# The gated delta rule in chunks of 128 tokens, with the transposed inverse of a level by transposing

## The chip, the cores and the metric

The kernel runs on one core of one Trainium2 chip. The metric is the device time of one launch in microseconds (us); the median of several executions is compared. The core has a matrix engine (TensorE, PE, with its weight loads listed as PEld), a vector engine (VectorE, DVE), a scalar engine (ScalarE, ACT), GpSimd (POOL) and SyncE (SP), which issues the DMAs here. The engines run their own queues in order and wait for each other by semaphores.

## The reference

The program is two blocks on 512 tokens of width 1024. The first is a depth-2 transformer-like block. The second has, beside a dilated window attention, a gated delta rule of 4 heads of width 128, which is what the change touches. Cut to that:

```python
def gated_delta_rule_chunked(q, k, v, g, beta):
    """S_t = exp(g_t) (I - beta_t k_t k_t^T) S_{t-1} + beta_t k_t v_t^T,  o_t = S_t^T q_t."""
    ...                                   # q, k, v, g, beta cut into chunks of CHUNK = 64
    gc = jnp.cumsum(g, axis=-1)           # within a chunk
    decay = jnp.exp(jnp.where(causal, gc[..., :, None] - gc[..., None, :], -jnp.inf))
    kb = k * beta[..., None]
    lower = jnp.where(strict, jnp.einsum('bhnid,bhnjd->bhnij', kb, k) * decay, 0.0)
    tmat = lax.linalg.triangular_solve(eye + lower, ...)        # the inverse
    u = jnp.einsum('bhnij,bhnjd->bhnid', tmat, v * beta[..., None])
    w = jnp.einsum('bhnij,bhnjd->bhnid', tmat, kb * jnp.exp(gc)[..., None])
    a_intra = jnp.where(causal, jnp.einsum('bhnid,bhnjd->bhnij', q, k) * decay, 0.0)

    def step(S, inp):                     # one chunk after the other
        qi, ki, ui, wi, ai, gci = inp
        v_new = ui - jnp.einsum('bhck,bhkv->bhcv', wi, S)
        o = jnp.einsum('bhck,bhkv->bhcv', qi * jnp.exp(gci)[..., None], S) + jnp.einsum('bhij,bhjv->bhiv', ai, v_new)
        glast = gci[..., -1]
        S = S * jnp.exp(glast)[..., None, None] + jnp.einsum(
            'bhck,bhcv->bhkv', ki * jnp.exp(glast[..., None] - gci)[..., None], v_new)
        return S, o
```

The size of a chunk is free: the recurrence in the docstring has the same answer for each.

## The kernel before

Everything is recorded first and then ordered by a planner (`Program.order`): it gives each instruction a guessed cost (`cost`, line 364), keeps a clock per engine, and takes for each engine the earliest-recorded instruction that can start, so that work recorded later fills the gaps of work recorded earlier. All instructions are issued from one line (684), so the names of tiles tell them apart. The planner also moves some elementwise work between DVE, POOL and ACT. `SLOW` is a table of guessed costs for the scan's products.

Large products are done as three single-pass products of high and low halves; the products of the delta rule are float32, which the profile lists as two instructions each. 512 tokens are four tiles `t` of 128; a tile named here has 128 partitions and 4 x 128 columns, one block for each `t`.

`block2` (line 1863) makes the second block: one head of the delta rule after the other (`dn_head`, line 1542), then the window attention (`swa`), a merge and the output product. For a head:
- `dnp` projects q, k, v and a gate; a convolution (`cy`), a silu (`sth`, `feat`) and norms follow, with transposes (`dtr`, a product with the identity).
- `gps` is the running sum of g over a chunk, `egl` its exponent at the end of a chunk. ET and E hold the decays, L the lower triangle, LT its transpose.
- The inverse of I + L is built by levels: D is the inverse of blocks of size s, DT its transpose. A level multiplies the part of LT between two blocks (LmT, by a mask `lvT`) with D, copies that to X, and subtracts X times DT from DT and DT times X from D. Five levels, with masks s = 2 to 32, give blocks of 64. The lines are 1652 to 1665; `mm4` does four products, one for each `t`.
- The scan goes over 8 chunks: `p1` is wT times the state S, `vn` is u minus p1, `dno` collects the output (a part from S by qeT, a part from vn by aT), `p2` is kd times vn and S is renewed with it. The trace lists p1 and p2 as p. Since a chunk has 64 tokens, the products use 64 rows or columns of the array: 128*64, 64*64 and 64*128 tiles.

Heads overlap: while a head runs its levels and scan, PE projects the next head (`dnp`), and behind the last heads the attention's projections (`pj`).

Of the kernel before, what the change touches and what calls it, by code (L numbers as in the profile page):

```python
# [10 lines left out]
F32 = mybir.dt.float32  # L11
F32R = mybir.dt.float32r
AF = mybir.ActivationFunctionType
OP = mybir.AluOpType
# [5 lines left out]
NEG = -1e30  # L20
# [40 lines left out]
def block_consts():  # L61
    f = np.float32
    p = np.arange(128)
    i, j = p[:, None], p[None, :]
    same = (i // 64) == (j // 64)
    U = (same & (i <= j)).astype(f)
    Bc = same.astype(f)
    causT = np.where(same & (j >= i), 0.0, NEG).astype(f)
    strict = (same & (i > j)).astype(f)

    def lv(s):
        return ((i // (2 * s) == j // (2 * s)) & (i % (2 * s) >= s) & (j % (2 * s) < s)).astype(f)
    lvT = np.stack([lv(s).T for s in (2, 4, 8, 16, 32)], 1)
    cur = np.where(j <= i, 0.0, NEG).astype(f)
    prev = np.where(j >= i, 0.0, NEG).astype(f)
    g2 = np.where((j <= i) & ((i - j) % 4 == 0), 0.0, NEG).astype(f)
    inv = (f(500000.0) ** (-np.arange(0, 32, 2, dtype=f) / f(32))).astype(f)
    ang = np.arange(TX, dtype=f)[:, None] * inv[None, :]
    c, s = np.cos(ang).astype(f), np.sin(ang).astype(f)
    C, S = np.concatenate([c, c], 1), np.concatenate([-s, s], 1)  # L80
    tabs = []
    for x in (C, S):
        tabs.append(np.stack([x.reshape(4, 128, 32).transpose(1, 0, 2), x.reshape(128, 4, 32)], 1))
    return [("U", U), ("Bc", Bc), ("causT", causT), ("strict", strict), ("nm0", -lv(1)), ("nm0T", -lv(1).T),
            ("lvT", lvT), ("cpc", np.concatenate([cur, prev, cur], 1)), ("g2", g2),
            ("cos", tabs[0]), ("sin", tabs[1]), ("e", np.full((128, 16), np.e, f))]
# [270 lines left out]
        return call  # L357

SLOW = {"p1": 0.27, "dno": 0.33, "p2": 0.42}


def cost(eng, fn, args, kw, n):

    views = [x for x in args if isinstance(x, View)]
    if eng == "sync":
        nbytes = 4 * int(np.prod([x.shape for x in args if hasattr(x, "shape")][0]))
        return max(nbytes / 360e3, 0.43), 2.2
    if eng == "tensor":  # L370
        if fn == "transpose":
            return 0.109, 0.1
        lhs, rhs = args[1], args[2]
        if rhs.dtype == F32:
            c = max(4 * n / 2400, 0.213) + 0.005
            if "tile_position" in kw:
                c /= 3.8
            elif args[0].tile.name in SLOW:
                c = SLOW[args[0].tile.name]
            elif lhs.shape[-1] == 64:  # L380
                c *= 0.63
            return c, 0.25
        return max(n * 0.000434 + 0.0095, 0.112), 0.12
    psum = any(v.tile.space == PSUM for v in views)
    ptrs = sum(isinstance(x, View) and x.shape[1:] == (1,) for x in args[2:] + (kw.get("scale"), kw.get("bias"))) if n > 1 else 0
    if eng == "vector":
        each = 0.0063 if fn == "reciprocal" else 0.00052 if fn == "tensor_scalar" and not psum else 0.00104
        return 0.07 + 0.06 * ptrs + n * each, 0.06
    if eng == "scalar":
        return 0.051 + 0.042 * (not psum) + 0.093 * (ptrs + ("accum_out" in kw)) + n * 0.000833, 0.06  # L390
    if kw.get("op") == OP.pow:
        return 0.3 + 0.165 * n, 0.1
    if fn == "memset":
        return 0.05 + n * 0.0004, 0.1
    slow = fn == "tensor_scalar" and isinstance(args[2], View)
    return 0.12 + n * (0.0025 if slow else 0.0022 if fn != "tensor_scalar" else 0.0009), 0.1
# [294 lines left out]
class Net:  # L691
# [337 lines left out]
    def swiglu(self, ws, z, n, ah, al, order="1657243"):  # L1029


        nc = self.nc
        X, Y, Z = (self.bank("gu")[:, :n] for _ in range(3))
        m1, u2, u3, g0 = (self.t2("gu")[:, :n] for _ in range(4))
        add = nc.vector.tensor_add
        for i in (int(x) for x in order):
            ps = {1: X, 2: X, 6: Y, 7: Y, 4: Y, 5: Z, 3: Z}[i]
            self.mm3(ps, [(ws[i][k], tuple(x[:, k] for x in z[i])) for k in range(4)], ((0, 0), (1, 0), (0, 1)),
# [5 lines left out]
            elif i == 6:  # L1044
                add(u2, m1, Y)
            elif i == 7:
                add(u3, m1, Y)
                add(u3, u3, Z)
            elif i == 4:
                add(m1, m1, Y)  # L1050
                nc.vector.tensor_mul(g0, g0, m1)
# [434 lines left out]
    def dn_stats(self, M, C, Pm):  # L1486
# [40 lines left out]
        gf = g.rearrange("p a b -> p (a b)")  # L1527
        nc.tensor.matmul(ps[:, 0, :], C["U"], gf, start=True, stop=True)
        nc.tensor.matmul(ps[:, 1, :], C["Bc"], gf, start=True, stop=True)
# [12 lines left out]
    def dn_head(self, h, M, C, Pm, st, ones):  # L1542
        nc = self.nc
# [4 lines left out]
        def t2(nm):  # L1548
            return self.t24(nm)

        def flat(x):
            return x.rearrange("p a b -> p (a b)")

        def bc(col):
            return col.unsqueeze(2).to_broadcast([128, 4, 128])

        def bt(m):
            return m.unsqueeze(1).to_broadcast([128, 4, 128])
# [5 lines left out]
        for i in range(4):  # L1564
            ps = self.bank("dnp")
            self.mm3(ps, [(ws[i][k], (zh[:, k, 0:TX], zl[:, k, 0:TX])) for k in range(KD)])
            dst = t2("feat")
            if i < 3:
# [3 lines left out]
                for j in (2, 1, 0):  # L1572
                    s = 3 - j
                    nc.vector.scalar_tensor_tensor(y[:, s:], ps[:, :TX - s], cw[:, j:j + 1], y[:, s:],
                                                   op0=OP.mult, op1=OP.add)
# [6 lines left out]
        def transposes(src):  # L1582
            tr = self.bank4("dtr")
            for t in range(4):
                nc.tensor.transpose(tr[:, t, :], src[:, t, :], ident)
            return tr

        def mm4(l, r):
            ps = self.bank4("dmm")
            for t in range(4):  # L1590
                nc.tensor.matmul(ps[:, t, :], l[:, t, :], r[:, t, :], start=True, stop=True)
            return ps
# [15 lines left out]
        rg = t2("rg")  # L1608
        nc.gpsimd.tensor_tensor(rg, bt(C["U"]), bc(gh), op=OP.mult)
        gps = self.bank4("gps")  # L1610
        nc.tensor.matmul(flat(gps), ones, flat(rg), start=True, stop=True)
        egl = self.sm.tile([128, 4, 2], F32, tag="egl", name="egl")
        nc.scalar.activation(egl, gps.rearrange("p t (c i) -> p t c i", c=2)[:, :, :, 63], AF.Exp)
        ET = t2("ET")
        nc.vector.tensor_tensor(ET, gps, bc(st["ngc"][:, h]), op=OP.add)
        nc.gpsimd.tensor_tensor(ET, ET, bt(C["causT"]), op=OP.add)
# [10 lines left out]
        for t in range(4):  # L1627
            nc.vector.scalar_tensor_tensor(L[:, t, :], G[:, t, :], st["beta"][:, h, t:t + 1], E[:, t, :],
                                           op0=OP.mult, op1=OP.mult)
        LT = t2("LT")  # L1630
        nc.scalar.copy(LT, transposes(L))
        D_, DT = t2("D"), t2("DT")
# [7 lines left out]
        aT = t2("aT")  # L1640
# [3 lines left out]
        qeT = t2("qeT")  # L1644
# [4 lines left out]
        kbe, kd = t2("kbe"), t2("kd")  # L1649
        nc.gpsimd.tensor_tensor(kbe, kn, bc(st["bge"][:, h]), op=OP.mult)  # L1650
        nc.gpsimd.tensor_tensor(kd, kn, bc(st["edl"][:, h]), op=OP.mult)
        for li in range(5):
            LmT = t2("LmT")
            nc.gpsimd.tensor_tensor(LmT, LT, bt(C["lvT"][:, li, :]), op=OP.mult)
            X = t2("X")
            nc.scalar.copy(X, mm4(LmT, D_))
            YT = mm4(X, DT)
            if li < 4:
                Y = mm4(DT, X)
                D2 = t2("D")  # L1660
                nc.vector.tensor_sub(D2, D_, Y)
                D_ = D2
            DT2 = t2("DT")
            nc.vector.tensor_sub(DT2, DT, YT)
            DT = DT2
        u, wT = t2("u"), t2("wT")
        nc.scalar.copy(u, mm4(DT, vb))
# [1 line left out]

        o = self.bank4("dno")  # L1670
        S = None
        for c in range(8):
            t, p0 = c // 2, 64 * (c % 2)
            ps = slice(p0, p0 + 64)
            if S is None:
                vn, vt = u, t
            else:
                p1 = self.bank("p1")[:, 0:128]
                nc.tensor.matmul(p1[ps, :], wT[:, t, ps], S, start=True, stop=True)
                vn, vt = M.tile([128, 1, 128], F32, tag="vn", name="vn", bufs=2), 0  # L1680
                nc.vector.tensor_sub(vn[ps, 0, :], u[ps, t, :], p1[ps, :])
                nc.tensor.matmul(o[ps, t, :], qeT[:, t, ps], S, start=True, stop=False)
            nc.tensor.matmul(o[ps, t, :], aT[ps, t, ps], vn[ps, vt, :], start=S is None, stop=True)
            if c < 7:
                p2 = self.bank("p2")[:, 0:128]
                nc.tensor.matmul(p2, kd[ps, t, :], vn[ps, vt, :], start=True, stop=True)
                S2 = M.tile([128, 128], F32, tag="S", name="S", bufs=2)
                if S is None:
                    nc.vector.tensor_copy(S2, p2)
                else:  # L1690
                    nc.vector.scalar_tensor_tensor(S2, S, egl[:, t, c % 2:c % 2 + 1], p2, op0=OP.mult, op1=OP.add)
                S = S2
        sq = t2("osq")
        nc.scalar.activation(sq, o, AF.Square)
# [394 lines left out]
```

## Time and profile before

| | |
|---|---|
| median of 3 runs | 3343.21 us (3342.05 to 3347.4) |
| the profiled execution | 3345.79 us, span 3344.0 us |
| mean granted clock of PE | 0.991 |
| PE busy | 98% of the span |
| DVE, ACT, POOL busy | 70%, 40%, 8% |
| DMA engines, q1 | 30.0% of the span, 334.61 MB |

The span is the time from the first to the last instruction of the profiled execution. In a timeline row the first number is the start, the second the busy time to the end of the last instruction of the row; matmuls are pipelined, so the difference between two starts, not the busy time, is what a row takes of PE. Tile shapes of PE stand as rows*columns of the array, then the shape that is written. A line such as `PE dmm L684 <- DVE D L684` reads: PE, about to write dmm, waited for DVE's write of D.

### The profile page before, as it was taken

What the parts mean: (1) busy time and instruction counts of PE and PEld (TensorE: products, weight loads), DVE (VectorE), ACT (ScalarE), POOL (GpSimd) and SP (SyncE); (2) the same over time, 40 slices, a digit from 0 to 9 for tenths busy, and PEclk for the clock granted to TensorE, in tenths of its full rate; (3) what the DMA queues carried; (4) which work ended last, traced back from release to release, by engine and by line L of the source; (5) the groups of instructions that cost most, each with busy time, mean ns of one, the idle gap of its engine ahead of it and who ended that gap; (6) DMA issues with size and microseconds to landing.
All of it is one profiled execution on the core that took longest, in us unless ns stands there. A gap on an engine that the chain in (4) does not pass through costs nothing.

```text
span 3344.0 us, 47695 instructions
## 1 busy us (share of the span) xinstructions
PE 3263.3 (98%) x18310; PEld 2812.8 (84%) x18310; DVE 2356.4 (70%) x4547; ACT 1341.6 (40%) x2764; POOL 268.3 (8%) x285
## 2 busy tenths in 40 slices
PE   7999999999999999999999999998999999999999
PEld 4889998777788999969999989767999887798987
DVE  6567769786766777887777795668889885666333
ACT  5333334554442333354333354345444442334431
POOL 1000001112000000110000012000000111321000
PEclk9999999999999999999999999998999999999999
DMA  7342113222543212352121232253333511112231
GB/s 254 108 170 70 65 68 127 86 89 102 180 157 115 75 58 75 111 187 73 63 75 59 91 118 88 98 189 101 102 107 108 167 57 45 51 45 66 82 95 63
DMA packets 161524, 337.66 MB, mean 101 GB/s; under 512 B 12256, under 2 KB 57696, under 8 KB 161168
## 3 DMA queue, kind: packets, MB, share of 16 engines
q1 hardware_dynamic: 161296, 334.61, 30.0%
q8 instruction: 144, 2.36, 0.3%
q14 instruction: 84, 0.69, 0.1%
HBM read 316.69 MB, written 17.87 MB: 100 GB/s over the span
## 4 chain that ended last, share of the span: by engine, by line
PE 85%; DVE 8%; DMA 3%; ACT 2%; issue 1%; SPq 0%; POOL 0%; POOLq 0%; ACTq 0%; DVEq 0%
PE gu L684 33%; PE dn L684 18%; PE pj L684 13%; PE pjf L684 5%; DVE h L684 2%; PE dnp L684 2%; PE ada L684 2%; PE dmm L684 2%; PE tr L684 1%; PE fin L684 1%; PE yb L684 1%; PE sc L684 1%; DMA raw<-in_ada_w 1%; PE pv L684 1%; PE ptr L684 1%
## 5 line engine op out<-in xcount | busy, mean ns | idle before, releaser
L684 ACT CAST whi<-raw 128x512 fp32r<-128x512 f32 x885 | 522.3, 620 | 673.1 <-PE gu L684 206.1
L684 DVE TENSOR_TENSOR wlo<-raw,whi 128x512 fp32r<-128x512 f32 x848 | 561.3, 687 | 223.2 <-ACT whi L684 210.1
L684 DVE TENSOR_TENSOR gu<-gu 128x384 f32<-128x384 f32 (+1 forms) x616 | 321.5, 522 | 276.8 <-PE gu L684 261.2
L684 DVE TENSOR_TENSOR h<-h,dn 128x512 f32<-128x512 f32 x404 | 273.6, 681 | 75.6 <-PE dn L684 74.7
L684 PE MATMUL dn<-wlo,ah 128*128 128x512 f32 x968 | 309.6, 394 | 0.0
L684 PE MATMUL dn<-whi,ah 128*128 128x512 f32 x968 | 308.8, 396 | 0.3 <-ACT ah L684 0.3
L684 PE MATMUL dn<-whi,al 128*128 128x512 f32 x968 | 304.9, 395 | 0.0
L684 PE MATMUL gu<-zh,whi 128*128 128x384 f32 (+1 forms) x1408 | 288.9, 326 | 13.1 <-DVE gu L684 7.4
L684 PE MATMUL gu<-zh,wlo 128*128 128x384 f32 (+1 forms) x1408 | 287.4, 322 | 0.0
L684 PE MATMUL gu<-zl,whi 128*128 128x384 f32 (+1 forms) x1408 | 283.2, 322 | 0.0
L684 PEld LDWEIGHTS gu<-zh,whi 128*128 128x128 f32 x1408 | 237.6, 189 | 36.8 <-DVE gu L684 8.7
L684 PEld LDWEIGHTS gu<-zh,wlo 128*128 128x128 f32 x1408 | 237.0, 189 | 0.9 <-issue 0.8
L684 PEld LDWEIGHTS gu<-zl,whi 128*128 128x128 f32 x1408 | 235.6, 189 | 1.0 <-issue 0.8
L684 PE MATMUL gu<-zxh,wlo 128*128 128x384 f32 (+1 forms) x1056 | 218.9, 326 | 5.2 <-DVE wlo L684 5.2
L684 ACT CAST whi<-ws 128x512 fp32r<-128x512 f32 x176 | 106.2, 620 | 280.1 <-PE dn L684 229.2
L684 PE MATMUL gu<-zxh,whi 128*128 128x384 f32 (+1 forms) x1056 | 214.6, 327 | 0.9 <-DVE gu L684 0.7
L684 PEld LDWEIGHTS dn<-wlo,ah 128*128 128x128 f32 x968 | 182.1, 188 | 39.5
L684 PE MATMUL gu<-zxl,whi 128*128 128x384 f32 (+1 forms) x1056 | 215.2, 325 | 0.0
L684 PEld LDWEIGHTS dn<-whi,al 128*128 128x128 f32 x968 | 181.8, 188 | 38.8 <-DVE al L684 0.2
L684 PEld LDWEIGHTS dn<-whi,ah 128*128 128x128 f32 x968 | 179.8, 189 | 39.1 <-ACT whi L684 3.4
L684 PE MATMUL pj<-whi,zh 128*128 128x512 f32 (+1 forms) x848 | 202.2, 373 | 8.2 <-ACT whi L684 3.1
L684 PEld LDWEIGHTS gu<-zxh,whi 128*128 128x128 f32 x1056 | 180.2, 189 | 18.8 <-ACT whi L684 4.7
(390 smaller groups left out, 5292.1 us busy)
## 6 DMA issues: line engine op xcount, KB each, us to landing
raw<-in_ffn_gu SPq DMA_DIRECT2D x176, 512.0 KB
raw<-in_ada_w SPq DMA_DIRECT2D x144, 512.0 KB
raw<-in_ffn_w_down SPq DMA_DIRECT2D x88, 512.0 KB
raw<-in_w_in SPq DMA_DIRECT2D x72, 512.0 KB
raw<-in_od_w_in SPq DMA_DIRECT2D x16, 512.0 KB
raw<-in_ev_w_in SPq DMA_DIRECT2D x14, 512.0 KB
gate<-gate SPq DMA_DIRECT2D x10, 512.0 KB
raw<-in_ev_w_out SPq DMA_DIRECT2D x8, 512.0 KB
```

The source lines that it names most:

```text
L684: getattr(self.real[o.eng], o.fn)(*[real(x) for x in o.args], **{k: real(v) for k, v in o.kw.items()})
```

## The change

A chunk has 128 tokens: the masks (`U`, `Bc`, `causT`, `strict`) cover whole blocks of 128, a sixth level with s = 64 is added, and the scan has four steps on whole tiles. In a level DT is no longer reduced by a product of its own: D is reduced, transposed on PE (`dtr`) and copied to DT by ACT; only the last level, which needs DT alone, still has the product with DT. The packed constants grow from 2448 to 2576 columns. The planner's `SLOW` table goes, so it guesses the scan's products like others.

```diff
     i, j = p[:, None], p[None, :]
-    same = (i // 64) == (j // 64)
-    U = (same & (i <= j)).astype(f)
-    Bc = same.astype(f)
-    causT = np.where(same & (j >= i), 0.0, NEG).astype(f)
-    strict = (same & (i > j)).astype(f)
+    U = (i <= j).astype(f)
+    Bc = np.ones((128, 128), f)
+    causT = np.where(j >= i, 0.0, NEG).astype(f)
+    strict = (i > j).astype(f)
...
-    lvT = np.stack([lv(s).T for s in (2, 4, 8, 16, 32)], 1)
+    lvT = np.stack([lv(s).T for s in (2, 4, 8, 16, 32, 64)], 1)
...
-SLOW = {"p1": 0.27, "dno": 0.33, "p2": 0.42}
...
-            elif args[0].tile.name in SLOW:
-                c = SLOW[args[0].tile.name]
...
-        egl = self.sm.tile([128, 4, 2], F32, tag="egl", name="egl")
-        nc.scalar.activation(egl, gps.rearrange("p t (c i) -> p t c i", c=2)[:, :, :, 63], AF.Exp)
+        egl = self.sm.tile([128, 4], F32, tag="egl", name="egl")
+        nc.scalar.activation(egl, gps[:, :, 127], AF.Exp)
...
-        for li in range(5):
+        for li in range(6):
             LmT = t2("LmT")
             nc.gpsimd.tensor_tensor(LmT, LT, bt(C["lvT"][:, li, :]), op=OP.mult)
             X = t2("X")
             nc.scalar.copy(X, mm4(LmT, D_))
-            YT = mm4(X, DT)
-            if li < 4:
-                Y = mm4(DT, X)
+            DT2 = t2("DT")
+            if li < 5:
                 D2 = t2("D")
-                nc.vector.tensor_sub(D2, D_, Y)
+                nc.vector.tensor_sub(D2, D_, mm4(DT, X))
                 D_ = D2
-            DT2 = t2("DT")
-            nc.vector.tensor_sub(DT2, DT, YT)
+                nc.scalar.copy(DT2, transposes(D_))
+            else:
+                nc.vector.tensor_sub(DT2, DT, mm4(X, DT))
             DT = DT2
...
-        for c in range(8):
-            t, p0 = c // 2, 64 * (c % 2)
-            ps = slice(p0, p0 + 64)
-            if S is None:
-                vn, vt = u, t
-            else:
+        for t in range(4):
+            vn = u[:, t, :]
+            if S is not None:
                 p1 = self.bank("p1")[:, 0:128]
-                nc.tensor.matmul(p1[ps, :], wT[:, t, ps], S, start=True, stop=True)
-                vn, vt = M.tile([128, 1, 128], F32, tag="vn", name="vn", bufs=2), 0
-                nc.vector.tensor_sub(vn[ps, 0, :], u[ps, t, :], p1[ps, :])
-                nc.tensor.matmul(o[ps, t, :], qeT[:, t, ps], S, start=True, stop=False)
-            nc.tensor.matmul(o[ps, t, :], aT[ps, t, ps], vn[ps, vt, :], start=S is None, stop=True)
-            if c < 7:
+                nc.tensor.matmul(p1, wT[:, t, :], S, start=True, stop=True)
+                vn = M.tile([128, 128], F32, tag="vn", name="vn", bufs=2)
+                nc.vector.tensor_sub(vn, u[:, t, :], p1)
+                nc.tensor.matmul(o[:, t, :], qeT[:, t, :], S, start=True, stop=False)
+            nc.tensor.matmul(o[:, t, :], aT[:, t, :], vn, start=S is None, stop=True)
+            if t < 3:
                 p2 = self.bank("p2")[:, 0:128]
-                nc.tensor.matmul(p2, kd[ps, t, :], vn[ps, vt, :], start=True, stop=True)
+                nc.tensor.matmul(p2, kd[:, t, :], vn, start=True, stop=True)
                 S2 = M.tile([128, 128], F32, tag="S", name="S", bufs=2)
                 if S is None:
                     nc.vector.tensor_copy(S2, p2)
                 else:
-                    nc.vector.scalar_tensor_tensor(S2, S, egl[:, t, c % 2:c % 2 + 1], p2, op0=OP.mult, op1=OP.add)
+                    nc.vector.scalar_tensor_tensor(S2, S, egl[:, t:t + 1], p2, op0=OP.mult, op1=OP.add)
                 S = S2
```

The planner orders the instructions anew from the first level of head 0 on; ahead of it PE's order is the same. PE at the first two levels of head 0, before (`dnp` are projections of head 1, in three kinds by the halves that they multiply):

```order
L684 MATMUL dmm<-D,LmT 128x128 x4
L684 MATMUL dnp<-zh,whi 128x512 x8
L684 MATMUL dmm<-DT,X 128x128 x4
L684 MATMUL dmm<-X,DT 128x128 x4
L684 MATMUL dnp<-zl,whi 128x512 x8
L684 MATMUL dnp<-zh,wlo 128x512
L684 MATMUL dmm<-D,LmT 128x128 x4
L684 MATMUL dnp<-zh,wlo 128x512 x7
```

and now:

```order
L677 MATMUL dmm<-D,LmT 128x128 x4
L677 MATMUL dnp<-zh,whi 128x512 x8
L677 MATMUL dmm<-X,DT 128x128 x4
L677 MATMUL dnp<-zl,whi 128x512 x8
L677 MATMUL dnp<-zh,wlo 128x512
L677 MATMUL dtr<-constA,D 128x128 x4
L677 MATMUL dmm<-D,LmT 128x128 x4
L677 MATMUL dnp<-zh,wlo 128x512 x7
L677 MATMUL dnp<-zh,whi 128x512 x2
```

The second product of the level (written as `dmm<-DT,X`) is gone, and four transposes of D stand ahead of the next level's first product, with eight or nine projections before and behind the level's second product.

PE in the scan of head 0, before (the number behind p tells its buffers apart), the fourth of eight steps and the start of the fifth:

```order
L684 MATMUL p_27026<-S,wT 64x128
L684 MATMUL dno<-S,qeT 64x128
L684 MATMUL dnp<-zh,wlo 128x512 x5
L684 MATMUL dno<-vn,aT 64x128
L684 MATMUL p_27041<-vn,kd 128x128
L684 MATMUL dnp<-zh,whi 128x512 x7
L684 MATMUL p_27055<-S,wT 64x128
L684 MATMUL dno<-S,qeT 64x128
```

and now, the second of four steps and the start of the third:

```order
L677 MATMUL p_27012<-S,wT 128x128
L677 MATMUL dno<-S,qeT 128x128
L677 MATMUL dnp<-zl,whi 128x512 x6
L677 MATMUL dnp<-zh,wlo 128x512
L677 MATMUL dno<-vn,aT 128x128
L677 MATMUL p_27030<-vn,kd 128x128
L677 MATMUL dnp<-zh,wlo 128x512 x7
L677 MATMUL p_27043<-S,wT 128x128
L677 MATMUL dno<-S,qeT 128x128
```

The products write 128 rows where they wrote 64 (p2 always wrote 128), there are half as many steps, and a step has up to 14 projections where it had 12.

## Rows read from the trace of the kernel before

**Rows 1.** The page: busy us, share of the span and instructions of each engine.

```profile
PE 3263.3 (98%) x18310; PEld 2812.8 (84%) x18310; DVE 2356.4 (70%) x4547; ACT 1341.6 (40%) x2764; POOL 268.3 (8%) x285
```

**Rows 2.** Windows: length, busy us of PE, PEld, DVE, ACT, POOL, clock, DMA.

```profile
2689.00:3000.00 311.00, 307.25 (x1739) 251.85 (x1738) 199.34 (x393) 100.89 (x199) 73.56 (x88) 1.00 0.14 43
...
3057.00:3090.00 33.00, 27.83 (x126) 23.91 (x125) 24.98 (x40) 13.64 (x44) 2.08 (x3) 0.84 0.25 80
```

**Rows 3.** Waits of PE, 2689 to 3057 us: total, times, longest.

```profile
PE dmm L684 <- DVE D L684: 1.7, 2, 1.5
PE pj L684 <- DVE of L684: 0.8, 1, 0.8
PE dmm L684 <- ACT X L684: 0.8, 1, 0.8
```

**Rows 4.** Timeline of PE: one scan step of head 0 (start us, us, what).

```profile
2756.70 0.43 PE L684 MATMUL p<-S,wT 128*64 128x128 f32 x2
2756.97 0.38 PE L684 MATMUL dno<-S,qeT 128*64 128x128 f32 x2
2757.28 1.45 PE L684 MATMUL dnp<-zh,wlo 128*128 128x512 f32 x5
2758.66 0.43 PE L684 MATMUL dno<-vn,aT 64*64 64x128 f32 x2
2759.02 0.48 PE L684 MATMUL p<-vn,kd 64*128 64x128 f32 x2
2759.43 1.86 PE L684 MATMUL dnp<-zh,whi 128*128 128x512 f32 x7
2761.23 0.43 PE L684 MATMUL p<-S,wT 128*64 128x128 f32 x2
```

**Rows 5.** Timeline of PE: transposes, whole-tile products, the first scan step.

```profile
2742.59 0.60 PE L684 MATMUL dtr<-constA,L 128*128 128x128 f32 x4
2743.03 0.83 PE L684 MATMUL dmm<-qnT,knT 128*128 128x128 f32 x6
2743.79 0.43 PE L684 MATMUL dno<-u,aT 64*64 64x128 f32 x2
2744.15 0.48 PE L684 MATMUL p<-u,kd 64*128 64x128 f32 x2
2744.56 0.49 PE L684 MATMUL dmm<-qnT,knT 128*128 128x128 f32 x2
...
2750.54 1.05 PE L684 MATMUL dmm<-DT,X 128*128 128x128 f32 x8
2751.43 0.61 PE L684 MATMUL dmm<-X,DT 128*128 128x128 f32 x4
```

**Rows 6.** Timeline of PE: a product of the levels among projections, head 0.

```profile
2704.41 1.98 PE L684 MATMUL dnp<-zh,wlo 128*128 128x512 f32 x8
2706.23 1.06 PE L684 MATMUL dmm<-D,LmT 128*128 128x128 f32 x8
2707.04 2.09 PE L684 MATMUL dnp<-zh,whi 128*128 128x512 f32 x8
2708.97 1.06 PE L684 MATMUL dmm<-DT,X 128*128 128x128 f32 x8
```

**Rows 7.** Windows of tile p alone (first row) and of tile dno (second).

```profile
2689.00:3000.00 311.00, 25.70 (x112) 13.59 (x112) 17.48 (x56) 1.00 0.14 43
2689.00:3000.00 311.00, 24.42 (x120) 12.90 (x120) 2.77 (x4) 2.39 (x4) 1.00 0.14 43
```

**Rows 8.** Groups: count, busy us, mean ns, idle before and releaser.

```profile
L684 ACT COPY X<-dmm 128x512 f32<-128x512 f32 x20 | 11.7, 585 | 29.3 <-PE dmm L684 29.3
L684 DVE TENSOR_TENSOR D<-D,dmm 128x512 f32<-128x512 f32 x16 | 10.8, 678 | 1.8 <-PE dmm L684 1.7
```

**Rows 9.** Timeline of PE after the heads: projections at a lower clock.

```profile
3067.99 3.80 PE L684 MATMUL pj<-whi,zh 128*128 128x512 f32 x8 [2.06 <-ACT swP L684]
3071.59 2.71 PE L684 MATMUL pj<-wlo,zh 128*128 128x512 f32 x6
```

## The prediction

> **What bounds the kernel now.** I read the page first: TensorE (PE) is busy 98% of the span, VectorE (DVE) 70%, ScalarE (ACT) 40% [rows 1]. An average says little of one stage, so I cut out the stage that the change touches, from the first `gps` product of head 0 to the end of the last head's scan. Of its 311 us PE is busy 307, at a granted clock of 1.00; DVE has 199 us of work there, ACT 101, and the DMA engines are 14% busy [rows 2]. The waits of PE in and just behind this stretch, three kinds, come to 3.3 us [rows 3]. So the four heads are chains of dependent work, but a chain is not what takes the time: the planner puts projections (`dnp` of the next head, `pj` of the attention behind it) between two links, and PE finds work. What counts is how much PE work there is, and what every instruction costs PE from its start to the next start. The busy time of one instruction is of no use for that, since neighbours overlap.
>
> **The scan: what goes.** A head's scan has 8 steps of 64 tokens. A full step is p1 and the state's share of `dno`, then the other share and p2. From one p1 to the next it is 4.53 us, and 12 projections lie in it [rows 4]. Eight projections step by 1.82 us where nothing else is near [rows 6], so 12 are 2.73 us, and the four scan products cost 1.80 us. The first step has two products only, 0.36 + 0.41 = 0.77 us [rows 5], and the eighth no p2, 1.80 - 0.41 = 1.39 us [rows 4]. A head: 0.77 + 6 x 1.80 + 1.39 = 12.96 us, four heads 51.8 us. The busy time of p and `dno` alone, 25.7 + 24.4 = 50.1 us, says about the same [rows 7].
>
> **The scan: what comes.** Four steps of 128 tokens have 3 p1, 3 + 4 `dno` and 3 p2: 13 products per head in place of 29, all of them 128 x 128 tiles with 128 columns moving. The trace has no scan product of this shape. The nearest row is the products of the levels, which have it: a set of four takes 0.89 us when another follows at once [rows 5], 0.2225 us each. Placed alone among projections a set takes 0.81 us and the eight projections behind it 1.93 instead of 1.82 [rows 6], so that an alternation costs 0.03 us. A head: 13 x 0.2225 + 7 alternations x 0.03 = 3.1 us, four heads 12.4 us. The upper bound is that a whole-tile product in the scan costs what the smaller one does, 1.80 / 4 = 0.45 us, which is 11 us more in four heads. I take 0.2225, because the price follows the tile's shape in the rows: the same pair of instructions starts its next neighbour after 0.22 us for a whole tile [rows 5], and after 0.27 to 0.41 us for 128*64, 64*64 and 64*128 tiles [rows 4]. Gain: 51.8 - 12.4 = 39.4 us.
>
> The Trainium skill, TensorEngine Tiling (Array Packing), Key Properties, says that a change of the tiling mode drains the engine, which agrees with the dear rows. Its Theoretical Speedup section speaks against this change, since it gives small tiles up to a factor of two; by that the 29 old products would cost an estimated 0.11 us each, 3.2 us a head, and the change would gain nothing in the scan. The rows have them at 0.27 to 0.41 us [rows 4] and never two side by side, so the measurement decides and this rule gets no chance of its own.
>
> **The levels.** Per head the inverse had 5 levels with 14 sets of four products, and has 6 levels with 12 sets now: -2 x 0.89 = -1.78 us. Five sets of transposes are new, 0.44 us each where a product follows [rows 5]: +2.20 us. They stand right ahead of the next product, so groups among projections go from 10 to 12: +0.06 us. Sum +0.48 us a head, +1.9 us in all. The transposing saves PE next to nothing over the product (0.44 against 0.89, for one more level); the gain is all in the scan.
>
> **Beside PE.** ACT gets some 24 copies of 0.585 us [rows 8], 14 us on 101. DVE loses 16 subtractions of DT, gains 4 of D at 0.68 us [rows 8] and 8 masks (some of them were on POOL), and does half the small scan operations: a little less than its 199 us. In a stage of some 273 us that is about 42% and 70%, and costs nothing as long as PE has fill. The two listings of PE show fill: 8 or 9 projections, 1.8 to 2.0 us, between the product that needs the mask and the one that needs X, and as many behind that one, where the copies of DT and X take 1.17 us and the subtraction 0.68 us [rows 8]. ACT's queue is in order: a copy of X waits behind that of DT and now and then behind a `sth`, which in turn waits for DVE; that is what uses the fill up. The first wait, 1.5 us for D [rows 3], stays: six masks instead of five stand ahead of D on DVE, but one convolution and the subtraction of DT less. I leave the 3.3 us of waits as they are. The larger constants are 64 KB more in one load, at 14% DMA. Rows of PE from the first transposed row sum (`strow`) to the end are the same in both, so the waits and the lower clock there [rows 2, 9] stay too.
>
> **Sum.** -39.4 + 1.9 = -37.5 us. The profiled execution took 3345.8 us, 2.6 us more than the median of 3343.2; its own sum gives 3308.3 us, and against the median I predict 3306 us, 1.1% less.
>
> **Rivals.**
> - Whole tiles are no cheaper in the scan: the price is that of accumulating and of weights that change with each product, not of the shape. Then 0.45 us a product, +11 us: 3317 us. Against it stands the 0.2225 us of level products, whose weights change too [rows 5].
> - The longer chain shows at each level once. Each level now has the subtraction, transposes and a second copy in a row, and the planner only guesses durations. The longest wait for X before was 0.8 us [rows 3]; one such wait in each of 24 levels is +19 us: 3325 us.
> - Slower than before, by one mechanism: the fill runs out between the links of the levels. Uncovered, a level costs PE the copies of DT and X and the subtraction, 2 x 0.585 + 0.68 = 1.85 us [rows 8], and three drains, 1.05 - 0.89 = 0.16 us each [rows 5]: 2.33 us, in 24 levels 56 us, 3362 us. It beats the gain from 37.5 / 24 = 1.56 us a level. Against it: the fill in the listing, and a scan that leaves more projections over.
> - PE's clock falls in the heads. After waits of 2 us the clock was at half in part of 3057 to 3090 us, mean 0.84 [rows 2], and 8 projections took 3.60 us [rows 9]. That is 33 x 0.16 = 5.3 us; once a head it is +21 us: 3327 us. Against it: 1.00 throughout the heads.
> - The change doesn't do what it says, as the projections that the scan no longer covers only move behind the heads and wait there for DVE and POOL: no change, 3343 us. Against it: DVE was 64% busy in the heads and PE still had its work.
>
> **How the numbers follow.** Forecast 76%; no cheaper tiles 8%; a wait per level 7%; half clock 4%; fill runs out 3%; no change 2%. The range reaches from 3302 us (the waits of 3.3 us go, the scan costs a little less) to 3318 us (the upper bound of the tile price): this holds the first two cases, 84%, less some scatter. A difference under 0.2%, 6.7 us, can't be told from none here. Faster by more than that are the forecast, the dear tiles, the waits and the clock, 95%; within it 2%; slower 3%.
>
> **What would show it.** After: 4.53 us between two p1 becomes 12 to 14 projections plus about 0.95 us for the four products; `dno` and p rows read 128*128, with 52 products instead of 116; the stage from the first `gps` to the first `strow` shrinks from 368 us (2689 to 3057) to about 331 us; PE's waits there stay under 6 us. Wrong would be steps of 0.4 us in the scan, or `dmm` and `dtr` waiting for ACT's DT or X and DVE's D by more than 10 us in sum.

## The result and the profile after

| | before | after |
|---|---|---|
| median | 3343.62 us (4 runs, 3342.05 to 3347.4) | 3301.24 us (4 runs, 3296.99 to 3304.87) |
| ratio, with its 95% interval | | 0.9869 [0.9856, 0.9881] |
| the profiled execution | 3345.79 us, span 3344.0 us | 3300.81 us, span 3299.0 us |

The kernel is 1.3% faster, as forecast in sign and place, but by 42.4 us and not 37.5: 0.8 us below the low end of the range. The four runs of the changed kernel spread over 8 us, so that 0.8 us alone says little; the stage below says more surely that the forecast was too small. The page of the changed kernel still has PE at 98% of the span (compare [rows 1]):

```profile
PE 3217.5 (98%) x18198; PEld 2795.8 (85%) x18198; DVE 2347.7 (71%) x4519; ACT 1356.7 (41%) x2788; POOL 254.1 (8%) x273
```

I call the time from the start of the first `gps` product to the start of the first `strow` transposition *the stage*. Before, it runs from 2689.0 to 3057.4 us, 368.4 us. The two groups of the changed kernel, each with its first and last start:

```profile
L677 PE MATMUL gps<-rg,ones x8: 590/592/594, 2688.7 to 2815.0; 128*128 128x512 f32 x8
L677 PE MATMUL strow<-constA,swM x12: 270/273/273, 3014.3 to 3031.0; 128*4 128x128 f32 x12
```

That is 325.6 us, 42.8 less; the forecast had 37.5 for it. The span is 45.0 less; where the other 2 us are is shown below.

Windows of the changed kernel: the heads, and the first 31 us behind the stage (busy us of PE, PEld, DVE, ACT, POOL, clock, DMA share, GB/s), to compare with [rows 2]:

```profile
2688.70:2960.00 271.30, 268.31 (x1646) 242.48 (x1644) 194.22 (x373) 117.22 (x231) 57.30 (x76) 1.00 0.16 49
...
3014.00:3045.00 31.00, 25.82 (x119) 22.68 (x118) 24.88 (x40) 13.05 (x44) 2.08 (x3) 0.83 0.26 84
```

In the heads PE is busy 268.3 of 271.3 us at full clock; DVE has 72% and ACT 43%, as worked out (70% and 42%). PE remains what is short. The waits of PE in the stage (total, times, longest), to compare with [rows 3]:

```profile
PE dtr L677 <- DVE D L677: 1.7, 1, 1.7
PE sws L677 <- DVE sn L677: 0.8, 1, 0.8
PE dtr L677 <- DVE feat L677: 0.4, 1, 0.4
```

The first wait for D stayed, the waits for X and for `of` are gone, one behind the attention's `sn` and one for `feat` came. In sum they are 2.9 us; before it was 3.5 us, the 3.3 of [rows 3] and a fourth wait of 0.2 us for `vn`.

One scan step of head 0 in the timeline of PE (start, busy us, what), to compare with [rows 4]:

```profile
2749.84 0.38 PE L677 MATMUL p<-S,wT 128*128 128x128 f32 x2
2750.05 0.39 PE L677 MATMUL dno<-S,qeT 128*128 128x128 f32 x2
2750.20 1.63 PE L677 MATMUL dnp<-zl,whi 128*128 128x512 f32 x6
2751.66 0.39 PE L677 MATMUL dnp<-zh,wlo 128*128 128x512 f32 x1
2751.89 0.38 PE L677 MATMUL dno<-vn,aT 128*128 128x128 f32 x2
2752.11 0.39 PE L677 MATMUL p<-vn,kd 128*128 128x128 f32 x2
2752.26 1.86 PE L677 MATMUL dnp<-zh,wlo 128*128 128x512 f32 x7
2753.95 0.38 PE L677 MATMUL p<-S,wT 128*128 128x128 f32 x2
```

From p1 to p1 it is 4.11 us with 14 projections; at the forecast's 0.2275 us each these are 3.19 us, and the four products take 0.93 us, where the forecast said 0.95. The next instruction starts 0.15 us (a projection) to 0.22 us after a product, not 0.27 to 0.41. The windows of tile p and of tile `dno` alone, to compare with [rows 7]:

```profile
2688.70:3000.00 311.30, 9.25 (x48) 7.95 (x48) 6.79 (x22) 0.53 (x2) 1.00 0.18 57
2688.70:3000.00 311.30, 10.78 (x56) 9.47 (x56) 2.75 (x4) 2.39 (x4) 1.00 0.18 57
```

48 and 56 listed instructions instead of 112 and 120, 20.0 us busy instead of 50.1.

The first level of head 0, timeline of PE, to compare with [rows 6]:

```profile
2708.67 1.05 PE L677 MATMUL dmm<-X,DT 128*128 128x128 f32 x8
2709.48 2.08 PE L677 MATMUL dnp<-zl,whi 128*128 128x512 f32 x8
2711.40 0.39 PE L677 MATMUL dnp<-zh,wlo 128*128 128x512 f32 x1
2713.48 0.66 PE L677 MATMUL dtr<-constA,D 128*128 128x128 f32 x4 [1.69 <-DVE D L677]
2713.97 1.06 PE L677 MATMUL dmm<-D,LmT 128*128 128x128 f32 x8
2714.78 1.40 PE L677 MATMUL dnp<-zh,wlo 128*128 128x512 f32 x5
```

The transposes come behind D's subtraction and take 0.49 us here, after a wait of 1.69 us; the wait of [rows 3] (1.5 us) has moved from the level's product to its transposes. The copies on ACT (count, busy us, mean ns, idle before), to compare with [rows 8], cost what was said and hold nobody up:

```profile
L677 ACT COPY X<-dmm 128x512 f32<-128x512 f32 x23 | 13.5, 586 | 7.3 <-PE dmm L677 6.8 <-DVE D L677 0.3 <-issue 0.2
L677 ACT COPY DT<-dtr 128x512 f32<-128x512 f32 x19 | 11.1, 586 | 23.2 <-PE dtr L677 22.1 <-DVE DT L677 1.0
```

### The profile page after: what moved, and what is told of

The parts are those of the page before. It is cut to its first block, busy times and chain, and to the rows that moved or that the text cites. A ratio compares the mean times of both kernels' runs of the same rounds, so it can differ in the third digit from the quotient of the medians.

```text
span 3299.0 us, 47460 instructions
## 1 busy us (share of the span) xinstructions
PE 3217.5 (98%) x18198; PEld 2795.8 (85%) x18198; DVE 2347.7 (71%) x4519; ACT 1356.7 (41%) x2788; POOL 254.1 (8%) x273
## 4 chain that ended last, share of the span: by engine, by line
PE 86%; DVE 8%; DMA 3%; ACT 2%; issue 1%; SPq 0%; POOL 0%; POOLq 0%; ACTq 0%; DVEq 0%
PE gu L677 33%; PE dn L677 18%; PE pj L677 13%; PE pjf L677 5%; DVE h L677 2%; PE ada L677 2%; PE dnp L677 2%; PE dmm L677 2%; PE tr L677 1%; PE fin L677 1%; PE sc L677 1%; PE yb L677 1%; DMA raw<-in_ada_w 1%; PE pv L677 1%; PE ptr L677 1%
## 5 line engine op out<-in xcount | busy, mean ns | idle before, releaser
L677 PE MATMUL gu<-zh,whi 128*128 128x384 f32 (+1 forms) x1408 | 288.3, 325 | 12.4 <-DVE gu L677 6.7
```

Source lines behind the costliest of these rows:

```text
L677: getattr(self.real[o.eng], o.fn)(*[real(x) for x in o.args], **{k: real(v) for k, v in o.kw.items()})
```

## Where the 42.8 us are

I added up, over the stage, what each PE instruction takes from its start to the next start beyond its undisturbed step: 0.232 us for a projection, 0.112 for an instruction of a product (two make one product), 0.109 for a transpose, 0.433 for a `gps` instruction. These are the medians between two of a kind in the stage of the kernel before. The sum beyond is split into what stands at scan products (their joints with each other and with both neighbours) and the rest (other joints, and waits). The first column is the difference of the two starts, as above.

| kernel | stage us | scan instructions | beyond, at the scan | beyond, the rest |
|---|---|---|---|---|
| before | 368.4 | 232 | 27.0 | 9.6 |
| after | 325.6 | 104 | 0.3 | 6.3 |

The scan cost 232 x 0.112 + 27.0 = 53.0 us and costs 104 x 0.112 + 0.3 = 11.9 us: 41.1 less. In the levels 64 product instructions went (576 to 512, -7.2 us) and 80 transposes came (144 to 224, +8.7 us): 1.5 us more. The rest fell by 3.3 us. Together -41.1 + 1.5 - 3.3 = -42.9 us.

To which column a joint goes is a choice. If the step behind a scan product always counts to the scan, whatever stands there, the table reads 27.8 and 8.8 before, 0.4 and 6.2 after: the scan fell by 41.8 us and the rest by 2.6. So the division is good to under 1 us; the total does not depend on it.

## The experiments

Every ratio is to the kernel before, run beside the variant: it took 3349.84 us beside the first three variants and the changed kernel's repeat, 3350.91 us beside the undone transposing, the order without the table and the last try, and 3347.12 us beside the order with the table. The stage is compared with 368.4 or 325.6 us.

The theory: PE has work throughout, so each part is worth what it puts on PE or takes off it, and the scan's price comes from the tile's shape. The rivals: it comes from accumulating and changing weights; or the longer chain of a level shows; or the new order of instructions is what gained the extra 5 us.

**Only the shape: eight steps on whole tiles.** The kernel before, every scan product on all 128 rows and columns:

```diff
-                nc.tensor.matmul(p1[ps, :], wT[:, t, ps], S, start=True, stop=True)
+                nc.tensor.matmul(p1, wT[:, t, :], S, start=True, stop=True)
...
-                nc.tensor.matmul(o[ps, t, :], qeT[:, t, ps], S, start=True, stop=False)
+                nc.tensor.matmul(o[:, t, :], qeT[:, t, :], S, start=True, stop=False)
-            nc.tensor.matmul(o[ps, t, :], aT[ps, t, ps], vn[ps, vt, :], start=S is None, stop=True)
+            nc.tensor.matmul(o[:, t, :], aT[:, t, :], vn[:, vt, :], start=S is None, stop=True)
```

(and p2 and vn likewise; lines that stay are left out. PE's order in the stage is the same as before, instruction by instruction, so this run changes the shape and nothing else of PE's work.)

> The kernel before, chunks of 64 and eight steps kept, but every product of the scan made on the whole 128*128 tile (the other half of each step's rows is written over, so the output is not the reference's; nothing else is left out). The count stays 116 products, only the tile's shape changes. Theory (the price follows the shape, since a change of shape empties the array): 29 products at 0.2225 us and some 15 alternations at 0.03 us, 6.9 us a head instead of 12.96, so -24 us in all: 3319 us; steps between a product's two instructions 0.11 us, none of 0.16 or 0.2 us. Rival (accumulating and new weights set the price, whatever the shape): no change, 3344 us, and the whole gain of the change came from half as many steps.

Measured: 3322.17 us, ratio to the kernel before 0.992 [0.9906, 0.9935]; the stage 344.4 us (2690.4 to 3034.8), 24.0 less, with the same 232 scan instructions. A step of head 0 in the timeline of PE:

```profile
2756.62 0.38 PE L684 MATMUL p<-S,wT 128*128 128x128 f32 x2
2756.84 0.39 PE L684 MATMUL dno<-S,qeT 128*128 128x128 f32 x2
2756.99 1.40 PE L684 MATMUL dnp<-zh,wlo 128*128 128x512 f32 x5
2758.22 0.38 PE L684 MATMUL dno<-vn,aT 128*128 128x128 f32 x2
2758.44 0.39 PE L684 MATMUL p<-vn,kd 128*128 128x128 f32 x2
2758.58 1.86 PE L684 MATMUL dnp<-zh,whi 128*128 128x512 f32 x7
2760.29 0.38 PE L684 MATMUL p<-S,wT 128*128 128x128 f32 x2
```

The step has the same 12 projections as in [rows 4] and is 3.67 us long instead of 4.53. The excess at the scan fell from 27.0 to 3.5 us. So more than half of the gain needs no longer chunk at all. (This variant leaves out what would keep the two halves apart; a whole one with chunks of 64 on whole tiles was not built.) What was dear is the change of tile shape rather than the small tile: in the kernel before, `dno<-S,qeT` follows p1 in the same 128*64 shape, and from p1's second instruction to it, and from its first to its second, it is 0.109 or 0.110 us in all 28 cases, as little as for a whole tile. The dear steps are those at which the shape changes, and the one inside each product that comes first in a shape. That agrees with the Trainium skill, TensorEngine Tiling (Array Packing), Key Properties, by which a change of mode drains the engine. The factor of two that its section Theoretical Speedup gives to small tiles is not seen in the scan, where two small tiles never stood side by side. It is seen in the first block of the same trace, where small products of the attention come in pairs (timeline of PE, kernel before):

```profile
641.55 0.66 PE L684 MATMUL pv<-PT,v 128*64 128x128 f32 x8
642.14 0.44 PE L684 MATMUL ptr<-constA,P 128*128 128x128 f32 x2
```

Two of these instructions start 0.007 us apart and the next two 0.10 us later, so that two side by side step like one whole one. Whether the scan's small products could be paired, those of two heads for instance, no run tried.

**The price of a whole-tile product.** The changed kernel with products of the scan issued twice:

```diff
                 p1 = self.bank("p1")[:, 0:128]
                 nc.tensor.matmul(p1, wT[:, t, :], S, start=True, stop=True)
+                nc.tensor.matmul(p1, wT[:, t, :], S, start=True, stop=True)
```

(p2 and the state's share of `dno` likewise; lines that stay are left out.)

> The changed kernel with ten of each head's 13 scan products issued twice, the first result written over by the second (p1, p2 and the state's share of the output). 40 more whole-tile products: theory 0.2225 us each, +8.9 us on the changed kernel, 3310 us; rival (0.45 us each, as the small tiles): +18 us, 3319 us; if PE had spare time in the scan: +0.

The expectation has a count wrong: nine products of a head are issued twice, not ten, since there are three p1, three p2 and three shares of `dno` from the state; 36 in all, which the theory puts at 8.0 us and the rival at 16. Measured: 3315.48 us, ratio 0.99 [0.9885, 0.9914], against 0.9868 [0.9853, 0.9883] of the changed kernel beside it; the stage 336.6 us, 11.0 more. The 72 more instructions at 0.112 us are 8.1 us, the excess at the scan is 0.3 us as it was, and the rest grew by 3 us. Of these, waits are 0.7 us more, and 1.4 us come from a stretch at 2922 us in which the granted clock was at half (a mean of 0.72 from 2921 to 2927 us). The waits of PE in this run:

```profile
PE dtr L677 <- DVE D L677: 2.0, 2, 1.7
PE sws L677 <- ACT swP L677: 1.6, 1, 1.6
```

The whole stage grew by 11.0 us, between the two forecasts, and it is the steps at the scan that decide: 0.2225 us holds, and 0.45 falls.

**Only the transposing.** The kernel before, with the level's lines of the changed one (`if li < 4`).

```diff
-            YT = mm4(X, DT)
+            DT2 = t2("DT")
             if li < 4:
-                Y = mm4(DT, X)
                 D2 = t2("D")
-                nc.vector.tensor_sub(D2, D_, Y)
+                nc.vector.tensor_sub(D2, D_, mm4(DT, X))
                 D_ = D2
-            DT2 = t2("DT")
-            nc.vector.tensor_sub(DT2, DT, YT)
+                nc.scalar.copy(DT2, transposes(D_))
+            else:
+                nc.vector.tensor_sub(DT2, DT, mm4(X, DT))
```

> The kernel before with only the transposing: chunks of 64, five levels, eight steps on small tiles, but DT by transposes and a copy in the first four levels. Theory (PE work counts): 16 sets of four products (0.89 us) become 16 sets of transposes (0.44 us): -7.2 us, 3336 us. Rival (the longer chain of subtraction, transposes and copy shows, 0.8 us a level): +13 - 7 = +6 us, 3349 us.

Measured: 3335.27 us, ratio 0.996 [0.9947, 0.9973]; the stage 357.0 us, 11.4 less. 128 product instructions less and 64 transposes more are -14.3 + 7.0 = -7.4 us, as expected. The other 4 us, which the theory did not have, stand in joints and waits: the excess at the scan is 24.3 instead of 27.0 and the rest 8.3 instead of 9.6. The order is new there, and fewer scan products stand beside projections (85 such joints instead of 108); that this is the cause was not tried by itself. Two of PE's waits in this run:

```profile
PE dtr L684 <- DVE D L684: 2.0, 2, 1.6
PE dmm L684 <- ACT X L684: 0.2, 1, 0.2
```

The wait for D is 0.3 us longer in sum than in [rows 3], that for X is 0.6 shorter, and none is for a copy of DT. So the longer chain does not cost 0.8 us a level.

**Only the chunk.** The changed kernel with DT by a product in each of six levels (the level's lines of before, with `if li < 5`).

> The changed kernel with the transposing undone: chunks of 128, six levels, four steps, but DT reduced by a product of its own in each level, as before. Theory (PE work counts): 20 sets of transposes (0.44 us) become 20 sets of products (0.89 us), +9 us on the changed kernel: 3310 us, -33 us on the kernel before. Rival (the chain through transposes and copies shows in the changed kernel): less than +9 us, down to -5 us.

Measured: 3316.47 us, ratio 0.9905 [0.9889, 0.992]; the stage 335.1 us, 9.5 more than the changed kernel. 160 product instructions more and 80 transposes less are 17.9 - 8.7 = +9.2 us, and the excess is 2.7 us at the scan and 4.2 in the rest. With this the two parts stand in a square:

| stage us | DT by a product | DT by transposing |
|---|---|---|
| chunks of 64 | 368.4 | 357.0 |
| chunks of 128 | 335.1 | 325.6 |

The chunk, with the removal of the table that goes with it here, is worth 33.3 us with products and 31.4 with transposing; the transposing is worth 11.4 with five levels and 9.5 with six.

**Only the order.** The kernel before without the planner's table `SLOW`, and the changed kernel with it put back: the work is that of its neighbour, only the order of the instructions differs.

```diff
-            elif args[0].tile.name in SLOW:
-                c = SLOW[args[0].tile.name]
```

> The kernel before with the planner's table of guessed scan costs taken out, so that only the order changes. Theory (the order hides the chain either way): within 2 us of the kernel before, 3342 to 3346 us. Rival (the 5 us beyond the forecast came from the new order): 3338 us.

> The changed kernel with the planner's old table of guessed scan costs (0.27, 0.33, 0.42 us) put back, so that it guesses the whole-tile products too dear and orders the instructions anew; the work is the same. Theory (a new order alone moves waits and joints of PE by some 3 us either way, and that is what the forecast left out): the stage from the first gps product to the first strow 323 to 330 us beside 325.5 us, with the scan and level products at the same price. Rival (the order has no part in it): 325 to 326 us.

Measured: without the table the kernel before takes 3355.48 us, ratio 1.0014 [1.0004, 1.0024], the stage 371.2 us, 2.8 more: the order shows, where the theory had within 2 us, and it costs, where the rival had a gain. The changed kernel with the table takes 3312.48 us, ratio 0.9889 [0.987, 0.9908], the stage 327.6 us, 2.0 more. Two of the waits of PE without the table, kernel before:

```profile
PE dmm L682 <- DVE D L682: 4.9, 2, 3.4
PE pj L682 <- DVE of L682: 0.8, 1, 0.8
```

One wait for D is 3.4 us now; it had been two of 1.5 and less [rows 3]. Behind it the granted clock fell to half, which it did nowhere in the stage before (window 2861 to 2866 us, columns as in [rows 2]):

```profile
2861.00:2866.00 5.00, 4.46 (x23) 4.32 (x24) 4.62 (x9) 1.70 (x3) 1.01 (x1) 0.66 0.00 0
```

By the steps that stretch cost 1.4 us. Two of the waits with the table, changed kernel:

```profile
PE sws L682 <- ACT swP L682: 2.3, 1, 2.3
PE dtr L682 <- DVE D L682: 1.7, 1, 1.7
```

Here 2.3 us for an exponent of the attention are new, and the clock fell again (a mean of 0.72 from 2917 to 2923 us, 1.5 us by the steps). So the order alone moves the stage by two to three us with not one instruction of work changed. The rest, 9.6 us before and 6.3 after, is 12.2 us without the table and 8.6 in the changed kernel with it. With the table in both kernels the stage gains 40.8 us and the rest falls by 1.0; without it in both it gains 45.6 and the rest falls by 5.9. Each kernel was measured in the better of its two orders. The removal of the table by itself is no part of the gain: in the old kernel it costs.

**The changed kernel again**, in one series with the first three:

> The changed kernel as it is, beside the others on the same chip. 3301 us, -42 us on the kernel before; from the first gps product to the first strow 325 to 326 us against 368 us; the rest moves by up to 4 us with what the clock does behind the heads.

Measured: 3305.04 us, the kernel before 3349.84 there, ratio 0.9868 [0.9853, 0.9883]. Its first and last starts:

```profile
L677 PE MATMUL gps<-rg,ones x8: 590/592/594, 2694.6 to 2820.9; 128*128 128x512 f32 x8
L677 PE MATMUL strow<-constA,swM x12: 270/272/273, 3020.1 to 3036.8; 128*4 128x128 f32 x12
```

The stage is 325.5 us once more; what differs is where it starts, 2694.6 instead of 2688.7 us, although the instructions ahead of it are the same.

**A try at more.** Behind the stage PE waits 5.2 us in three waits and runs at half clock for a while [rows 2, 9], in both kernels. I recorded the value projection of the second group ahead of the third group's scores:

```diff
+        v1 = None
         for g in range(3):
+            if g == 2:
+                v1 = proj(1, 5128, v_tile)
             scores(g, qk(g, 2056, "qrow", qsc[:, g:g + 1]), qk(g, 3592, "krow", Pm["kcol"][:, g:g + 1]))
...
-            vs = v0 if v0 and g == 0 else proj(g, 5128, v_tile)
+            vs = (v0, v1)[g] if g < 2 else proj(g, 5128, v_tile)
```

> The changed kernel with the value projection of the attention's second group recorded ahead of the third group's scores, so that there is PE work while the last scores wait. Theory (5.2 us of waits behind the heads and the low clock after them are the last loss in this stage): waits there fall, and with them the stretch at half clock: 3 to 9 us less than the changed kernel, 3292 to 3298 us. Rival (the weights of that projection come no earlier, or its buffers block others): no change or slower, 3301 us or more.

Measured: 3308.66 us, ratio 0.988 [0.9862, 0.9898], no better than the changed kernel. The planner took the projection as fill inside the stage, which is 350.5 us with 96 projections more (22.3 us), 2.6 us longer than it should be, and the three waits behind the stage are what they were:

```profile
PE tr L677 <- DVE sn L677: 2.3, 1, 2.3
PE pj L677 <- ACT swP L677: 2.1, 1, 2.1
PE strow L677 <- ACT qk L677: 0.8, 1, 0.8
```

## Why the forecast was right and where it failed

- **PE's work bounds the stage, and the chain hides.** Right. The waits of PE in the stage are 2.9 us, and no product waits for a copy of DT or X.
- **What the scan cost.** Mis-sized: 51.8 us against 53.0 (53.8 by the other way of counting). One step was taken as the price of all, and over all steps the joints came to more. That the busy time of 50.1 us came near was luck: it is 20.0 us now, and the price is 11.9.
- **What it costs now.** 12.4 against 11.9 us. The choice of the nearest shape, 0.2225 us a product, was right, and the doubling and the eight whole-tile steps show it. The reason was near but not quite it: not every small tile was dear, only those where the shape changed, as `dno` behind p1 shows. An alternation costs less than the 0.03 us that I put in.
- **The levels.** +1.9 against +1.5 us. But the sentence that the transposing saves next to nothing gave the wrong picture: it is true only of both edits together. The sixth level would have cost 12 x 0.89 = 10.7 us with products (three sets in four heads), and the transposing is worth 9.5.
- **The waits and joints left as they are.** This is the step that failed: the forecast put the change of this term at nothing, and it measured -3.3 us. The listed waits fell only from 3.5 to 2.9 us, so most of it is small joints, and these the forecast priced nowhere but at the scan and for two more groups a head. The order was new from the first level on, and much of this term hangs on the order: it falls by 1.0 us with the table in both kernels and by 5.9 without it in both. Nothing in the forecast could tell which. Why the order as made gave just 3.3 us is not shown joint by joint. The runs that change the order alone move the stage by +2.8 and +2.0 us, so a term that I set to zero has a spread of some 3 us, and I did not put that into the range: the low end of 3302 us took in the waits of [rows 3] and some 0.4 us more for a cheaper scan. The scan, 1.7 us, the levels, 0.4, and this term, 3.3, are the 5.4 us between 37.5 and 42.9. All three went the same way; none made up for another.
- **The tail stays.** The instructions did and the waits did, but the profiled executions differ by 1.9 us there. In the one of before a second stretch ran below full clock:

```profile
3092.00:3097.00 5.00, 5.00 (x31) 4.34 (x31) 5.00 (x24) 3.20 (x8) 0.00 (x0) 0.74 0.00 0
```

and the same stretch of work in the changed kernel did not:

```profile
3049.00:3054.00 5.00, 5.00 (x45) 4.93 (x44) 5.00 (x25) 4.50 (x14) 0.00 (x0) 1.00 0.00 0
```

From the first `strow` to the end of the span it is 286.6 us before, 286.5 without the table, 284.7 in both executions of the changed kernel and 282.8 with eight whole-tile steps, PE's order there being the same in all. So the tail has its own spread of some 4 us, and the granted clock goes with it. In the first 40 us from the first `strow`, the kernel before, the changed one and eight whole-tile steps, in this order:

```profile
3057.40:3097.40 40.00, 34.83 (x164) 30.15 (x162) 31.35 (x69) 17.66 (x55) 2.08 (x3) 0.83 0.22 71
...
3014.30:3054.30 40.00, 34.82 (x180) 31.04 (x178) 31.74 (x71) 19.45 (x62) 2.08 (x3) 0.87 0.21 71
...
3034.80:3074.80 40.00, 34.83 (x197) 31.94 (x195) 32.22 (x73) 21.16 (x66) 2.08 (x3) 0.96 0.22 71
```

PE is as busy in all three, and gets less done where the mean clock is lower: 286.6 us at 0.83, 284.7 at 0.87, 282.8 at 0.96. What decides how long the clock stays low there, with the same instructions and the same waits, stays open. So the 1.9 us that the tail gave to the span were not forecast, and whether they are chance is not shown.

Of the rivals, dear whole tiles fell by the doubling, a wait per level and the fill that runs out by the list of waits, the half clock in the heads by the granted 1.00 (it did fall within the stage in three variants, at a price of 1.4 or 1.5 us each), and work that only moves behind the heads by the stage's end at 3014.3 us.

## What to carry to other kernels

Where PE is busy throughout, count its instructions by start-to-start steps, and price a change of tile shape separately: a few small-tile products among whole-tile ones cost here about as much again in joints as in work, and making them whole is worth trying, if the other half of the result can be kept out of the answer. Four products that only yield a transpose (0.89 us) are dearer than four transposes (0.44 us) and a copy, as long as the copying engine has time. And if a planner lays out the order anew, put a few us either way into the range, measured by a kernel in which only the planner's guesses are changed.

## What the runs showed that was not expected

- In three of a step's four products on 64 rows or columns the first instruction took 0.16 or 0.21 us to its partner's start, against 0.112 for a whole tile (the fourth, `dno` behind p1 in the same shape, 0.109), and the projection behind paid again: 27.0 us beyond the steps in 116 products, 0.23 us each, as much as the product itself.
- Ahead of the stage the same instructions in the same order ended 2688.7 us and 2694.6 us after the start in two executions of the changed kernel. PE's idle time there is 69.5 us in the one and 72.3 in the other, and the granted clock was at half for 47.8 and 54.6 us. So an effect of some us is better read from the stage, which agreed within 0.1 us, than from the whole time.
